# Sums of float32r products written in descending order of columns, weights at other places modulo 128 bytes

## The chip, the cores and the metric

The kernel runs on one NeuronCore of a Trainium2 chip. The time is the device time of one execution, in microseconds (us). Before the change it is 1235.84 us, the median of three runs (1231.7, 1235.84 and 1236.56). An engine is named as in the profile: PE is TensorE's matmul, PEld its weight load, DVE VectorE, ACT ScalarE, POOL GpSimd, SP the queue that issues most DMAs.

## What is computed

Two residual layers run over 512 tokens of 1024 features, in float32. Layer 0 mixes tokens with a grouped complex state-space scan (S5) and a gated unit, layer 1 with forgetting attention of 16 heads (FoX). Behind each stands a gated feed-forward layer (1024 to 2 x 2816 to 1024) with a causal convolution of width 3 on one branch. Each part is modulated by shift, scale and gate that are worked out from a conditioning vector. The change bears on the large products alone:

```python
u = h @ w_in                                  # S5, and y @ w_glu, y @ w_out
proj = h @ w_in                               # FoX: q, k, v and forget logits; o @ w_out
up = h @ w_up                                 # ConvFFN, both layers
a, b = jnp.split(up, 2, axis=-1)
return (jax.nn.silu(a_conv) * b) @ w_down
```

## The kernel before

**Layout.** Activations lie transposed: 128 features on the partitions, 512 tokens along them, eight such tiles (KT) for 1024 features. A tile of output features is 128 wide, so a product of 128 x 1024 weights with the activations is 8 steps (`k`) that add into one sum in PSUM.

**Three products for one.** Most large products are made in float32r from numbers split in two parts, `hi` (rounded by a copy on ACT, line 277) and `lo` (the rest, a subtraction on DVE, line 278). `mms` (line 294) issues three matmuls a step: hi x hi, hi x lo, lo x hi; all three times the k steps add into the same sum. The weights are the stationary operand, so each matmul has its own weight load of 128 columns, and the activations are the moving operand of 512 or 256 columns. `split` loads a tile of weights by DMA (queue of SP), makes its two parts, and `weights` hands out the k slices.

**Where weights lie.** `part_of` takes a slot of the pool and starts the weights `aside` elements of 4 bytes behind its beginning. A slot has `ROOM` = 9 x 128 elements, which is 36 x 128 bytes, so `aside` alone tells how one tile's weights lie modulo 128 bytes against another's. It is 0 by default; `ASIDE` = 16 elements is 64 bytes.

**`product`** (line 298 and on) runs over the output tiles `ms` and has three parts. The *head* makes several tiles at once, k outside, tiles inside, over `halves`: with two halves every matmul is 256 columns wide (the first tiles of both feed-forward layers, three tiles each), with one half 512 (the first four tiles of `fox`'s output product). The *middle* makes one tile after the other at 512 columns. The *tail* makes its tiles for the first half of the tokens and then for the second, 256 columns wide, with weights 64 bytes aside, so that the norm that follows can start on the first half. Each finished sum goes to `evac`, a function of the caller that reads it from PSUM: `gated` in the feed-forward layer, `add_residual` (line 362) behind w_down and the mixers' outputs, `project` (queries and keys), `glu`.

**`quarters`** (line 510 and on) replaces two tiles of `w_up` by seven products of half size in the manner of Strassen and Winograd: `times` (line 550) issues 4 k steps x 3 matmuls of 256 columns; its weights are sums and differences of blocks of `w_up`, split like the others and laid 64 bytes aside. `copy` (line 557, ACT) takes an interim sum out of PSUM, and the sums of two are made on DVE (line 518). It is used for 33 of the 44 pairs of tiles.

**`fox_values`** makes the values the other way round: tokens' activations are the stationary operand and the weights, 64 bytes aside, the moving one (line 1361), 256 columns, or 272 with the forget logits.

**What sets the order.** Each engine takes its instructions in the order in which the program issues them. PE runs through the products one behind the other; `mm` and `aux` hold four banks of PSUM each, so a sum can be read while the next is made. Weights are split ahead: five slots of `w_hi` and `w_lo`, three of `raw`. Between the products, `tick` issues pieces of the modulation of later parts (DMA of SP or POOL, reduction on DVE), and in `fox` `step=self.unit` issues pieces of attention between the k steps.

Other float32r products lie outside the functions that the change touches: `glu_head` (line 1198), the attention logits (line 1470), the weighing of values (line 1520). The S5 part's products are float32 without the split.

Of the kernel before, what the change touches and what calls it, by code (L numbers as in the profile page):

```python
# [8 lines left out]
F32 = mybir.dt.float32  # L9
F32R = mybir.dt.float32r  # L10
I32 = mybir.dt.int32
AF = mybir.ActivationFunctionType
ALU = mybir.AluOpType
# [4 lines left out]
P = 128  # L18
D = 1024
KT = D // P  # L20
S = 512
# [9 lines left out]
NH = 16  # L31
HD = 64
# [5 lines left out]
RAW, WB = 3, 5  # L38
# [23 lines left out]


ROOM, ASIDE = 9 * P, 16


def part_of(pool, shape, name, tag, bufs, aside=0):

    _, n, w = shape
    t = pool.tile([P, ROOM if bufs == WB else n * w + P], F32R, name=name, tag=tag, bufs=bufs)  # L70
    return t[:, aside:aside + n * w].rearrange("p (n w) -> p n w", w=w)


class Trunk:
# [223 lines left out]
    def product(self, w, ms, nk, x, evac, head=0, tail=0, after=None, ticks=0, halves=HALVES, tail_pool=(), first=None, step=None):  # L298


        ms = list(ms)
        full = slice(0, S)
        if head:
            wk = first or {m: self.weights(w[m], nk) for m in ms[:head]}
            ps = {m: self.mm.tile([P, S], F32, name="mmp") for m in ms[:head]}
            for c in halves:
                for k in range(nk):
                    for m in ms[:head]:
                        self.mms(ps[m][:, c], wk[m], x, k, nk, c)
                    self.finish_norm((k + 1) * head)  # L310
                    if step:
                        step(3)
            for m in ms[:head]:
                evac(m, ps[m], full)
                self.tick(ticks)
        for m in ms[head:len(ms) - tail]:
            wk = self.weights(w[m], nk)
            ps = self.mm.tile([P, S], F32, name="mmp")
            for k in range(nk):
                self.mms(ps, wk, x, k, nk, full)  # L320
                if step:
                    step()
            evac(m, ps, full)
            self.tick(ticks)
        if tail:
            last = ms[len(ms) - tail:]
            wk = {m: self.weights(w[m], nk, *tail_pool, aside=ASIDE) for m in last}
            for c in HALVES:
                for m in last:
                    if c is HALVES[1] and m == last[tail // 2]:  # L330
                        rb = self.rms_rows(y)
                    ps = self.mm.tile([P, S // 2], F32, name="mmp")
                    for k in range(nk):
                        self.mms(ps, wk[m], x, k, nk, c)
                    evac(m, ps, c)
                if c is HALVES[0]:
                    y = after[0](c)
                else:
                    y2 = after[0](c)
                    after[1](HALVES[0], y, rb)  # L340
            self.pending = lambda: after[1](HALVES[1], y2)
# [168 lines left out]
    def quarters(self, pool, l, f, x, finish):  # L510

        nc = self.nc
        H, N = KT // 2, S // 2
        t1, t2 = HALVES
        a, b = (self.raw([P, KT, P], self.io["w_up"][l][2 * f + j]) for j in range(2))
        a11, a12, a21, a22 = a[:, :H], a[:, H:], b[:, :H], b[:, H:]
        c, d = (pool.tile([P, 2, H, P], F32, name="sums", bufs=2) for _ in range(2))
        sub = lambda o, u, v, op=ALU.subtract: nc.vector.tensor_tensor(o, u, v, op)  # L518
        w = {}
        copied = self.copied  # L520

        def parts(src, names, *where):
            hi, lo = (
                pool.tile([P, H * P + P], F32R, name=n, tag="e" + n)[:, ASIDE:ASIDE + H * P].rearrange("p (n w) -> p n w", w=P)
                if where else part_of(self.wpool, [P, len(names) * H, P], n, n, WB, ASIDE)
                for n in ("w_hi", "w_lo")
            )
            with self.behind(*copied):
                self.put_parts(hi, lo, src)
            for j, n in enumerate(names):  # L530
                w[n] = hi[:, j * H:(j + 1) * H], lo[:, j * H:(j + 1) * H]
# [14 lines left out]
        def times(o, wn, xn, first=True):  # L546
            (whi, wlo), (xhi, xlo) = w[wn], xs[xn]
            for k in range(H):
                for n, (wt, xt) in enumerate(((whi, xhi), (whi, xlo), (wlo, xhi))):
                    self.last_mm = nc.tensor.matmul(  # L550
                        o, wt[:, k], xt[:, k], start=(first and k == 0 and n == 0), stop=(k == H - 1 and n == 2),
                        skip_group_check=True,
                    )

        def copy(o, last=False):
            t = self.tmp.tile([P, N], F32, name="nm_h", bufs=4)
            a = nc.scalar.activation(t, o, AF.Copy)  # L557
            if last:
                self.copied = [a.ins]
            return t  # L560
# [5 lines left out]
        c1 = copy(p1)  # L566
        times(p5, "s1", "t1")
        c5 = copy(p5)
        times(p2, "a12", "b21")
        sub(oa[:, t1], p2, c1, ALU.add)  # L570
        times(p1, "s2", "t2", False)
        c2 = copy(p1, True)
        times(p5, "s4", "b22", False)
        sub(oa[:, t2], p5, c2, ALU.add)
        finish(2 * f, oa, slice(0, S))
        times(p4, "a22", "t4")
        c4 = copy(p4)
        times(p1, "s3", "t3", False)
        sub(ob[:, t2], p1, c5, ALU.add)
        sub(ob[:, t1], p1, c4)  # L580
        finish(2 * f + 1, ob, slice(0, S))

    def ffn(self, i, l, x, nxt, ticks=0, plain=None):
# [96 lines left out]
class Ew:  # L680
# [29 lines left out]
    def sub(self, a, b, out=None):  # L710
        return self.tt(a, b, ALU.subtract, out)
# [577 lines left out]
class Kernel(S5):  # L1289
# [32 lines left out]
    def fox_values(self, pool, x):  # L1322
# [26 lines left out]
        def values(qs, blocks, w, aux=()):  # L1349
            todo = [(q, b) for q in qs for b in blocks]  # L1350
            ps = {
                k: self.aux.tile([P, S], F32, name="aux") if k in aux else self.mm.tile([P, S], F32, name="mmp")
                for k in todo
            }
            for k in range(KT):
                for q, b in todo:
                    hi, lo = w[q][k]
                    n = W if q else W + NH
                    tb = slice(b * P, (b + 1) * P)
                    for i, (xt, wt) in enumerate(((xhi, hi), (xhi, lo), (xlo, hi))):  # L1360
                        self.last_mm = nc.tensor.matmul(  # L1361
                            ps[q, b][:, :n], xt[:, k, tb], wt, start=(k == 0 and i == 0), stop=(k == KT - 1 and i == 2),
                        )
                self.finish_norm((k + 1) * len(todo))
            for q, b in todo:
                pv = ps[q, b][:, :W].rearrange("p (g r d) -> p g r d", r=2, d=HD)
                hi, lo = (self.v[:, 2 * q:2 * q + 2, b, :, t, :] for t in range(2))
                self.evac = [self.put_parts(hi, lo, pv).ins]
                if todo[0][0] == 0 and (b != 1 or q):
                    self.tick(1)  # L1370
                if q == 0:
                    nc.vector.tensor_tensor(ft[:, b, :], ps[q, b][:, W:W + NH], bf, ALU.add)

        w = load(range(2))
        self.tick(1)
# [265 lines left out]
```

## Time and profile before

| what | value |
|---|---|
| median of three runs | 1235.84 us (1231.7 to 1236.56) |
| the profiled execution | 1233.09 us |
| its span, first to last instruction | 1231.3 us |
| mean granted TensorE clock | 0.995 |
| DMA | 183.83 MB, mean 149 GB/s |
| matmuls by line 294, line 550, line 1361 | 2808, 2772, 384 |

How to read the profile: one execution was recorded by the hardware profiler. "L294 PE MATMUL mmp<-ghi,w_hi 128*128 128x512 f32 x312 | 121.8, 390" says that line 294 issued 312 matmuls with weights of 128 x 128 and a moving operand of 128 x 512, from the tiles ghi and w_hi into a sum named mmp; that PE was busy with them for 121.8 us (overlaps counted once) and that one took 390 ns on the average. Matmuls are pipelined: the next starts before the last has ended, so the distance of two starts is less than the duration. In the timeline the first column is the start in us from the span's beginning, the second the duration in us. In a row of windows the columns are the stretch, its length, then busy time and instructions of the engines (PE, PEld, DVE, ACT, POOL, or PE alone where the row is of one line's matmuls), the granted clock, the share of the DMA engines and GB/s. The chain of waits is followed back from the last instruction to whatever ended last before it.

### The profile page before, as it was taken

Reading aid. Unit: us, or ns where it says so; the run is one execution under the profiler, and the core shown is the slowest. Engines: PE = TensorE matmul, PEld = TensorE weight load, DVE = VectorE, ACT = ScalarE, POOL = GpSimd, SP = SyncE. Lnnn points to the kernel's source line nnn. Section 1 sums busy time; section 2 is a strip of 40 time slices with the busy share of each in tenths; the row PEclk is TensorE's granted clock in tenths of the full one; section 3 lists DMA queues with packets and bytes.
Section 4 is the critical chain, followed back from the end, with each engine's and each line's share of the span. In section 5 each row is a group of like instructions: output and inputs, shape, how many; then the busy total and the mean of one; then the engine's idle time right before and its main releaser. Section 6 shows DMA issues by size and latency. Waiting matters only on the chain.

```text
span 1231.3 us, 20566 instructions
## 1 busy us (share of the span) xinstructions
PE 1200.5 (97%) x7921; PEld 1031.2 (84%) x7921; DVE 1009.0 (82%) x1872; ACT 606.3 (49%) x1137; POOL 82.7 (7%) x143
## 2 busy tenths in 40 slices
PE   7999999999999999999999999999999999999997
PEld 2466678898989899889899887878989999999987
DVE  7988886779899988799687578876899887888865
ACT  3543465335544543445443565664366554545443
POOL 0000000100000000000000243430000000000000
PEclk9999999999999999999999999999999999999999
DMA  9776668530354544444445543432122332323231
GB/s 356 244 237 215 223 225 286 192 129 35 129 178 158 192 161 160 152 168 132 125 139 190 176 150 124 147 118 94 70 69 95 120 122 77 116 86 123 95 96 69
DMA packets 74385, 183.83 MB, mean 149 GB/s; under 512 B 23231, under 2 KB 25631, under 8 KB 73263
## 3 DMA queue, kind: packets, MB, share of 16 engines
q1 hardware_dynamic: 68239, 161.02, 38.4%
q0 software_dynamic: 5760, 20.97, 5.0%
q8 instruction: 62, 1.02, 0.3%
q10 hardware_dynamic: 288, 0.52, 0.1%
q14 instruction: 36, 0.29, 0.1%
HBM read 175.57 MB, written 6.92 MB: 148 GB/s over the span
## 4 chain that ended last, share of the span: by engine, by line
PE 75%; DVE 15%; DMA 4%; issue 3%; ACT 2%; POOL 0%; SPq 0%; DVEq 0%; ACTq 0%; POOLq 0%
PE mmp L294 32%; PE mmp L550 16%; PE aux L550 6%; DVE w_lo L278 5%; PE mmp L1169 4%; PE mmp L1361 2%; DMA rawd<-in_w_down 2%; PE aux L971 2%; PE mmp L1198 2%; PE aux L1060 1%; PE aux L1500 1%; PE mmp L205 1%; PE aux L1052 1%; DVE ada_raw L247 1%; PE mmp L1109 1%
## 5 line engine op out<-in xcount | busy, mean ns | idle before, releaser
L278 DVE TENSOR_TENSOR w_lo<-raw,w_hi 128x1024 fp32r<-128x1024 f32 (+4 forms) x173 | 183.3, 1065 | 35.4 <-ACT w_hi L277 34.8
L277 ACT ACTIVATE w_hi<-raw 128x1024 fp32r<-128x1024 f32 (+4 forms) x173 | 154.8, 905 | 101.5 <-PE mmp L294 53.1
L294 PE MATMUL mmp<-ghi,w_hi 128*128 128x512 f32 (+1 forms) x392 | 145.1, 370 | 0.0
L294 PE MATMUL mmp<-glo,w_hi 128*128 128x512 f32 (+1 forms) x392 | 144.8, 369 | 0.0
L294 PE MATMUL mmp<-ghi,w_lo 128*128 128x512 f32 (+1 forms) x392 | 144.5, 369 | 0.0
L294 PE MATMUL mmp<-a_hi,w_hi 128*128 128x512 f32 (+1 forms) x376 | 138.8, 372 | 1.5 <-ACT a_hi L433 1.5
L294 PE MATMUL mmp<-a_hi,w_lo 128*128 128x512 f32 (+1 forms) x376 | 136.6, 364 | 0.3 <-DVE w_lo L278 0.3
L294 PE MATMUL mmp<-a_lo,w_hi 128*128 128x512 f32 (+1 forms) x376 | 136.2, 363 | 0.0
L550 PE MATMUL mmp<-w_hi 128*128 128x256 f32 x396 | 111.4, 281 | 2.6 <-ACT nm_h L557 2.6
L550 PE MATMUL mmp<-w_hi,w_lo 128*128 128x256 f32 x396 | 111.1, 281 | 0.7 <-DVE w_lo L278 0.7
L550 PE MATMUL mmp<-w_lo,w_hi 128*128 128x256 f32 x396 | 111.1, 281 | 0.0
L557 ACT ACTIVATE nm_h<-mmp 128x256 f32<-128x256 f32 x99 | 37.9, 384 | 131.5 <-PE mmp L550 131.5
L278 DVE TENSOR_TENSOR w_lo<-sums,w_hi 128x1024 fp32r<-128x1024 f32 x74 | 90.1, 1219 | 0.3 <-ACT w_hi L277 0.2
L294 PEld LDWEIGHTS mmp<-ghi,w_lo 128*128 128x128 f32 x392 | 74.2, 189 | 12.7 <-DVE w_lo L278 0.4
L294 PEld LDWEIGHTS mmp<-glo,w_hi 128*128 128x128 f32 x392 | 74.5, 190 | 11.1
L277 ACT ACTIVATE w_hi<-sums 128x1024 fp32r<-128x1024 f32 x74 | 76.7, 1054 | 14.4 <-DVE sums L518 11.2
L294 PEld LDWEIGHTS mmp<-ghi,w_hi 128*128 128x128 f32 x392 | 74.2, 189 | 11.4
L294 PEld LDWEIGHTS mmp<-a_hi,w_hi 128*128 128x128 f32 x376 | 70.6, 189 | 13.8 <-issue 2.6
L294 PEld LDWEIGHTS mmp<-a_hi,w_lo 128*128 128x128 f32 x376 | 70.9, 189 | 12.3 <-DVE w_lo L278 1.3
L362 DVE SCALAR_TENSOR_TENSOR h<-mmp,par,h 128x512 f32<-128x512 f32 (+1 forms) x100 | 68.1, 683 | 15.3 <-PE mmp L294 15.0
L294 PEld LDWEIGHTS mmp<-a_lo,w_hi 128*128 128x128 f32 x376 | 71.1, 189 | 9.7
L550 PEld LDWEIGHTS mmp<-w_hi 128*128 128x128 f32 x396 | 74.3, 188 | 3.0 <-ACT nm_h L557 3.0
(317 smaller groups left out, 3092.6 us busy)
## 6 DMA issues: line engine op xcount, KB each, us to landing
raw<-in_w_up SPq DMA_DIRECT2D x88, 512.0 KB, 3.3
raw<-in_ada_w SPq DMA_DIRECT2D x40, 512.0 KB, 6.3
ada_raw<-in_ada_t POOLq DMA_DIRECT2D x40, 512.0 KB, 3.9
nf<-nfd SPq DMA_DIRECT2D x8, 1152.0 KB, 6.5
raw<-in_fox_qk SPq DMA_DIRECT2D x16, 512.0 KB, 3.6
raw<-in_w_down SPq DMA_DIRECT2D x24, 320.0 KB, 3.0
rawd<-in_w_down SPq DMA_DIRECT2D x24, 256.0 KB, 3.4
raw<-in_w_down SPq DMA_DIRECT2D x16, 384.0 KB, 3.3
```

Of the source, the lines that this page charges most:

```text
L205: self.last_mm = nc.tensor.matmul(ps[32 * qq:32 * qq + 32, :], self.sc32[:, k, :], w[:, q * S:(q + 1) * S], start=(step is steps[0]), stop ...
L247: nc.vector.tensor_tensor_reduce(w, w, self.c_row, 1.0, 0.0, ALU.mult, ALU.add, sums[:, j:j + 1])
L277: nc.scalar.activation(hi, src, AF.Copy)
L278: return nc.vector.tensor_tensor(lo, src, hi.bitcast(F32), ALU.subtract)
L294: self.last_mm = self.nc.tensor.matmul(o, wt, xt[:, cols], start=(k == 0 and n == 0), stop=(k == nk - 1 and n == 2),)
L362: add = self.nc.vector.scalar_tensor_tensor(self.h[:, m, cols], ps, self.par[i][:, 16 + m:17 + m], self.h[:, m, cols], op0=ALU.mult, op1=A ...
L550: self.last_mm = nc.tensor.matmul(o, wt[:, k], xt[:, k], start=(first and k == 0 and n == 0), stop=(k == H - 1 and n == 2), skip_group_che ...
L557: a = nc.scalar.activation(t, o, AF.Copy)
L971: nc.tensor.matmul(ps[g2][:, j, cols], x[rows, a + j, r].rearrange("p c j -> p (c j)"), self.rr[rows, planes, q, :], start=(j == 0 and r = ...
L1169: nc.tensor.matmul(ps, w[m][:, k, :], x[:, k], start=(k == 0), stop=(k == KT - 1))
L1198: nc.tensor.matmul(gps[m], wt, xt[:, k], start=(k == 0 and part == 0 and xt is yhi), stop=(k == KT - 1 and part == 1))
L1361: self.last_mm = nc.tensor.matmul(ps[q, b][:, :n], xt[:, k, tb], wt, start=(k == 0 and i == 0), stop=(k == KT - 1 and i == 2),)
```

## The change

`back` gives a view of a sum's columns from the last to the first. The matmuls now write through that view: the first column of the moving operand goes to the last column of the PSUM tile, the second to the one before, and so on. Every reader of such a sum reads it through the same view. It is done for the middle and the tail of `product`, for its head if there are two halves, for `quarters` and for `fox_values`. The head with one half (in `fox`) and the products outside these functions stay as they were. The moving operands and the weights are read in the old order.

`PLACES` are eight distances in elements: 4, 8, 16, 32, 48, 64, 80 and 96 bytes. The middle of `product` takes the one of its output tile's number modulo 8 (it was 0), `quarters` that of its pair's number modulo 8 (it was 64 bytes, and stays so for the one block that has a slot of its own). The head with two halves goes from 0 to 64 bytes.

```diff
--- before.py
+++ after.py
@@ -62,6 +62,7 @@
 
 
 ROOM, ASIDE = 9 * P, 16
+PLACES = (1, 2, 4, 8, 12, 16, 20, 24)
 
 
 def part_of(pool, shape, name, tag, bufs, aside=0):
@@ -69,6 +70,11 @@
     _, n, w = shape
     t = pool.tile([P, ROOM if bufs == WB else n * w + P], F32R, name=name, tag=tag, bufs=bufs)
     return t[:, aside:aside + n * w].rearrange("p (n w) -> p n w", w=w)
+
+
+def back(t):
+
+    return t[:, ::-1]
 
 
 class Trunk:
@@ -301,8 +307,11 @@
         ms = list(ms)
         full = slice(0, S)
         if head:
-            wk = first or {m: self.weights(w[m], nk) for m in ms[:head]}
+            two = len(halves) == 2
+            wk = first or {m: self.weights(w[m], nk, aside=ASIDE if two else 0) for m in ms[:head]}
             ps = {m: self.mm.tile([P, S], F32, name="mmp") for m in ms[:head]}
+            if two:
+                ps = {m: back(t) for m, t in ps.items()}
             for c in halves:
                 for k in range(nk):
                     for m in ms[:head]:
@@ -314,8 +323,8 @@
                 evac(m, ps[m], full)
                 self.tick(ticks)
         for m in ms[head:len(ms) - tail]:
-            wk = self.weights(w[m], nk)
-            ps = self.mm.tile([P, S], F32, name="mmp")
+            wk = self.weights(w[m], nk, aside=PLACES[m % 8])
+            ps = back(self.mm.tile([P, S], F32, name="mmp"))
             for k in range(nk):
                 self.mms(ps, wk, x, k, nk, full)
                 if step:
@@ -331,8 +340,8 @@
                         rb = self.rms_rows(y)
                     ps = self.mm.tile([P, S // 2], F32, name="mmp")
                     for k in range(nk):
-                        self.mms(ps, wk[m], x, k, nk, c)
-                    evac(m, ps, c)
+                        self.mms(back(ps), wk[m], x, k, nk, c)
+                    evac(m, back(ps), c)
                 if c is HALVES[0]:
                     y = after[0](c)
                 else:
@@ -522,7 +531,7 @@
         def parts(src, names, *where):
             hi, lo = (
                 pool.tile([P, H * P + P], F32R, name=n, tag="e" + n)[:, ASIDE:ASIDE + H * P].rearrange("p (n w) -> p n w", w=P)
-                if where else part_of(self.wpool, [P, len(names) * H, P], n, n, WB, ASIDE)
+                if where else part_of(self.wpool, [P, len(names) * H, P], n, n, WB, PLACES[f % 8])
                 for n in ("w_hi", "w_lo")
             )
             with self.behind(*copied):
@@ -548,13 +557,13 @@
             for k in range(H):
                 for n, (wt, xt) in enumerate(((whi, xhi), (whi, xlo), (wlo, xhi))):
                     self.last_mm = nc.tensor.matmul(
-                        o, wt[:, k], xt[:, k], start=(first and k == 0 and n == 0), stop=(k == H - 1 and n == 2),
+                        back(o), wt[:, k], xt[:, k], start=(first and k == 0 and n == 0), stop=(k == H - 1 and n == 2),
                         skip_group_check=True,
                     )
 
         def copy(o, last=False):
             t = self.tmp.tile([P, N], F32, name="nm_h", bufs=4)
-            a = nc.scalar.activation(t, o, AF.Copy)
+            a = nc.scalar.activation(t, back(o), AF.Copy)
             if last:
                 self.copied = [a.ins]
             return t
@@ -567,17 +576,17 @@
         times(p5, "s1", "t1")
         c5 = copy(p5)
         times(p2, "a12", "b21")
-        sub(oa[:, t1], p2, c1, ALU.add)
+        sub(oa[:, t1], back(p2), c1, ALU.add)
         times(p1, "s2", "t2", False)
         c2 = copy(p1, True)
         times(p5, "s4", "b22", False)
-        sub(oa[:, t2], p5, c2, ALU.add)
+        sub(oa[:, t2], back(p5), c2, ALU.add)
         finish(2 * f, oa, slice(0, S))
         times(p4, "a22", "t4")
         c4 = copy(p4)
         times(p1, "s3", "t3", False)
-        sub(ob[:, t2], p1, c5, ALU.add)
-        sub(ob[:, t1], p1, c4)
+        sub(ob[:, t2], back(p1), c5, ALU.add)
+        sub(ob[:, t1], back(p1), c4)
         finish(2 * f + 1, ob, slice(0, S))
 
     def ffn(self, i, l, x, nxt, ticks=0, plain=None):
@@ -1359,17 +1368,18 @@
                     tb = slice(b * P, (b + 1) * P)
                     for i, (xt, wt) in enumerate(((xhi, hi), (xhi, lo), (xlo, hi))):
                         self.last_mm = nc.tensor.matmul(
-                            ps[q, b][:, :n], xt[:, k, tb], wt, start=(k == 0 and i == 0), stop=(k == KT - 1 and i == 2),
+                            back(ps[q, b][:, :n]), xt[:, k, tb], wt, start=(k == 0 and i == 0), stop=(k == KT - 1 and i == 2),
                         )
                 self.finish_norm((k + 1) * len(todo))
             for q, b in todo:
-                pv = ps[q, b][:, :W].rearrange("p (g r d) -> p g r d", r=2, d=HD)
+                sums = back(ps[q, b][:, :W if q else W + NH])
+                pv = sums[:, :W].rearrange("p (g r d) -> p g r d", r=2, d=HD)
                 hi, lo = (self.v[:, 2 * q:2 * q + 2, b, :, t, :] for t in range(2))
                 self.evac = [self.put_parts(hi, lo, pv).ins]
                 if todo[0][0] == 0 and (b != 1 or q):
                     self.tick(1)
                 if q == 0:
-                    nc.vector.tensor_tensor(ft[:, b, :], ps[q, b][:, W:W + NH], bf, ALU.add)
+                    nc.vector.tensor_tensor(ft[:, b, :], sums[:, W:W + NH], bf, ALU.add)
 
         w = load(range(2))
         self.tick(1)
```

## What the change does to the time: the prediction

> **What bounds the kernel now.** I read the page first, its busy shares and its chain, and then the starts of consecutive products in the timeline.
>
> ```profile
> span 1231.3 us, 20566 instructions
> PE 1200.5 (97%) x7921; PEld 1031.2 (84%) x7921; DVE 1009.0 (82%) x1872; ACT 606.3 (49%) x1137; POOL 82.7 (7%) x143
> PE 75%; DVE 15%; DMA 4%; issue 3%; ACT 2%; POOL 0%; SPq 0%; DVEq 0%; ACTq 0%; POOLq 0%
> PE mmp L294 32%; PE mmp L550 16%; PE aux L550 6%; DVE w_lo L278 5%; PE mmp L1169 4%; PE mmp L1361 2%; DMA rawd<-in_w_down 2%; PE aux L971 2%; PE mmp L1198 2%; PE aux L1060 1%; PE aux L1500 1%; PE mmp L205 1%; PE aux L1052 1%; DVE ada_raw L247 1%; PE mmp L1109 1%
> ```
>
> TensorE makes 75% of the chain, and lines 294, 550 and 1361, which the change touches, make 56%. So what counts is how far apart two products start, and not the mean duration of one, which holds a tail that the next product overlaps. The timeline gives the distance: here are the first and the last row of stretches without a stall.
>
> ```profile
> 294.96 0.39 PE L294 MATMUL mmp<-a_hi,w_lo 128*128 128x512 f32 x1
> ...
> 297.91 0.39 PE L294 MATMUL mmp<-a_hi,w_hi 128*128 128x512 f32 x1
> ...
> 269.72 0.28 PE L294 MATMUL mmp<-a_hi,w_hi 128*128 128x256 f32 x1
> ...
> 272.48 0.28 PE L294 MATMUL mmp<-a_hi,w_lo 128*128 128x256 f32 x1
> ...
> 469.67 0.28 PE L550 MATMUL mmp<-w_hi 128*128 128x256 f32 x1
> ...
> 473.91 0.28 PE L550 MATMUL mmp<-w_hi 128*128 128x256 f32 x1
> ...
> 619.66 0.28 PE L294 MATMUL mmp<-ghi,w_hi 128*128 128x256 f32 x1
> ...
> 623.28 0.28 PE L294 MATMUL mmp<-ghi,w_lo 128*128 128x256 f32 x1
> ```
>
> The first pair spans 13 steps of 512 columns: 2.95/13 = 226.9 ns. The other pairs are 256 columns wide. Line 294 in the head of `product`, weights at place 0: 23 steps, 2.76/23 = 120.0 ns. Line 550 in `quarters`, weights 64 bytes aside: 36 steps, 4.24/36 = 117.8 ns. Line 294 in the tail, 64 bytes aside too: 32 steps, 3.62/32 = 113.1 ns. The last two have the same place and different distances, so place is not the only thing that sets them; but no stretch at place 0 in this head settles under 120.
>
> A second reading tells what part of this is TensorE's own pace. The granted clock falls to half for a moment (0.50, third figure from the right in the first row below), and there the distance is:
>
> ```profile
> 615.90:617.00 1.10, 1.10 (x8) 1.10 (x6) 0.00 (x0) 1.10 (x2) 0.00 (x0) 0.50 0.00 0
> ...
> 617.87 0.41 PE L294 MATMUL mmp<-ghi,w_lo 128*128 128x256 f32 x1
> ...
> 618.94 0.39 PE L294 MATMUL mmp<-glo,w_hi 128*128 128x256 f32 x1
> ```
>
> Five steps, 1.07/5 = 214 ns for 256 columns: 0.836 ns a column. Were the pace TensorE's alone, the full clock would give half of that, 107 ns for 256 and 214 for 512. The rows show 113 to 120 and 227. So **some 6% of every product is lost to something that does not slow with TensorE's clock**: a store that is read or written. The trace does not say which: the moving operand, the weights (both SBUF) or the sums (PSUM).
>
> **The change part by part.** It adds, removes and moves no instruction, no DMA and no wait; each of its edits changes an address pattern. The products that it touches:
>
> ```profile
> L294 PE MATMUL mmp<-ghi,w_hi 128*128 128x512 f32 x312 | 121.8, 390 | 0.0
> ...
> L294 PE MATMUL mmp<-zhi,w_lo 128*128 128x512 f32 x48 | 18.7, 389 | 0.0
> 0.00:1231.00 1231.00, 584.49 (x2808) 1.00 0.44 149
> 0.00:1231.00 1231.00, 332.68 (x2772) 1.00 0.44 149
> 0.00:1231.00 1231.00, 46.31 (x384) 1.00 0.44 149
> ```
>
> The three last rows are all products of lines 294, 550 and 1361. Of line 294's 2808, the groups kept apart by shape (the first and the last of eleven rows of 512 columns into `mm` stand above; three more into `aux` have 8 each) give 2064 + 24 of 512 columns; 96 of these are the head of `fox` (one half, not touched) and 24 are the fifth glu tile (not in `product`). That leaves 1968 of 512 columns, at 227 ns 447 us, and 720 + 2772 + 384 = 3876 of about 256, at 118 ns 457 us: **904 us of a span of 1231 hang on the distance**, 1% of it being 9 us.
>
> *Sums written backwards.* Nothing in this trace is written by TensorE with a negative step, so the price is bounded from both sides. From below: if the 6% is lost where the sums are written, and direction is its cause, the distances fall to 214 and 107 ns: 1968 x 13 + 3876 x 11 ns = 68 us saved. From above: if sums that do not ascend go in one column at a time at the slow pace of 0.836 ns a column, 512 columns take 428 ns and 256 take 214: 1968 x 201 + 3876 x 96 ns = 768 us lost. I take zero, for two reasons in the rows. Weights moved by 64 bytes change the distance, so the loss reacts to an SBUF address, and that says reading more than writing. And the moving operand is still read forwards: SBUF sees the old order.
>
> The Trainium skill, page "PSUM — Partial Sum Buffer", section "Specifications (TRN2)", speaks against the change: PSUM has 8-byte lines and any access pattern that isn't contiguous slows matmuls significantly. Page "Advanced Engine Details and Errata", section "Memory Cachelines", words it as every two consecutive elements being contiguous, and by that wording a backward pair still shares a line. No row here shows a backward or strided sum of any width; by the first wording the upper bound above would hold, by the second the zero.
>
> *Readers of the sums.* ACT and DVE now read PSUM backwards. The nearest rows are a PSUM read in steps of eight elements and one in order, both 128x512 on ACT:
>
> ```profile
> L1171 ACT ACTIVATE uf<-mmp 128x512 f32<-128x512 f32 x7 | 4.2, 603 | 10.7 <-issue 10.6
> L1420 ACT ACTIVATE hi<-mmp 128x512 fp32r<-128x512 f32 x8 | 4.6, 579 | 0.0
> L557 ACT ACTIVATE nm_h<-mmp 128x256 f32<-128x256 f32 x99 | 37.9, 384 | 131.5 <-PE mmp L550 131.5
> L557 ACT ACTIVATE nm_h<-aux 128x256 f32<-128x256 f32 x33 | 12.1, 368 | 1.7 <-PE aux L550 1.5
> PE mmp L550 <- ACT nm_h L557: 2.6, 2, 2.4
> ```
>
> A step of eight costs 603 - 579 = 24 ns. From zero to 24 ns on each of line 557's 132 copies (99 + 33) is 0 to 3 us of ACT, which is 49% busy, and PE waits for that line 2 times in all, 2.6 us. I take 0, for DVE's reads too, of which no row has a step: four banks of `mm` and the next product cover it. Without that cover it would be 3 us.
>
> *Places.* Weights of `product`'s middle tiles go from place 0 to eight places from 4 to 96 bytes, those of `quarters` from 64 bytes to the same eight, the head in two halves from 0 to 64. Bounds for `quarters` are the rows above: 113.1 (gain 4.7) to 120.0 (loss 2.2) from 117.8, times 2772: -13 to +6 us. At 512 columns a settled stretch has 226.9; behind a switch from 256 to 512 columns, stretches like this one are slower for six products:
>
> ```profile
> 443.24 0.40 PE L294 MATMUL mmp<-ghi,w_hi 128*128 128x512 f32 x1
> ...
> 444.40 0.39 PE L294 MATMUL mmp<-ghi,w_lo 128*128 128x512 f32 x1
> ```
>
> Five steps, 1.16/5 = 232 ns. If a place held the 512-wide products there, each would lose 5 ns: 1968 x 5 = +10 us at most; the least is 0. I take half of `quarters`' tiles at 120 and half unchanged, 1386 x 2.2 ns = +3 us, since two of the eight places (4 and 8 bytes) lie nearest to 0 and the others between, and 0 for the 512-wide ones, because they settled at 226.9 while their weights lay at 0, where the 256-wide head has its worst distance. The head in two halves gains 2.2 ns on 288 products (3 tiles, 8 steps, 3 products, 2 halves, 2 layers): -0.6 us.
>
> **Sum.** 0 + 0 + 3 - 0.6 = +2.4 us on the profiled execution of 1233.1 us (span 1231.3 and 1.8 around it). That execution was 2.7 us under the median of 1235.84, so against the median the forecast is **1238 us**: no change that a measurement shows. What it can tell apart from none is about 0.5%, 6 us.
>
> **Rivals.**
>
> *The backward order removes the loss: faster.* For it: the 6% does not follow TensorE's clock, and the sum's order is the one thing changed in all touched products. Against it: the place of weights moves the distance too. Price: up to 68 us. But 107 ns needs weight loads to keep up; the nearest row is a run of 64-column products, each with a load of 128 columns:
>
> ```profile
> 174.79 0.94 PE L1052 MATMUL aux<-u,t 128*128 128x64 f32 x7
> 175.54 0.48 PE L1198 MATMUL mmp<-a_hi,w_hi 128*128 128x512 f32 x1
> ...
> 307.00:500.00 193.00, 192.41 (x1250) 175.27 (x1249) 174.10 (x270) 92.34 (x147) 11.68 (x22) 1.00 0.46 159
> ```
>
> Seven in 0.75 us is 107 ns, so loads just keep up. The stretch from 307 to 500 us has DVE at 174 of 193 us: with PE 11 us shorter (845 x 11 and 405 x 13 ns would be 15 us) DVE begins to be late with `w_lo` and `sums`. I count 70% of the gain: -47 us, **1190 us**, between 1172 and 1215.
>
> *The places hold the products in their slow patterns: slower.* Place: the settled stretches of lines 294 and 550. Price: +10 us (512 columns at 232 ns) and +6 us (256 at 120): **1252 us**, and up to 1270 if places off the grid of 16 bytes cost as much again. It decides from the point where six of eight places act like place 0. For it: the 120 ns row. Against it: 512-wide products return to 226.9 after six.
>
> *Sums go in one column at a time: much slower.* The price is the upper bound, 768 us, on 1236: **some 2000 us**, less what hides behind it. For it speaks that TensorE's writes in this trace all ascend without a step, so nothing shows that another order keeps the pace. Against it: backward neighbours are as near as forward ones. The skill's first wording, above, is this rival.
>
> **How the numbers follow.** No change in the pace, 1238 us with its own range of 1224 to 1250 (the -13 and +6 of `quarters`, the +10): 0.37. The loss goes away, 1190: 0.29. Places slow, 1252: 0.14. One column at a time, 2000: 0.20. The range leaves out the last alone and takes in the ends of the others: 1172 to 1270. Faster by over 0.5% (under 1229.7) takes the second case and 0.07 of the first: 0.36. Slower (over 1242) takes the third and fourth and 0.13 of the first: 0.47. Within: 0.17.
>
> **What would show it.** Right: 226.9 ns steady in `product`'s 512-wide tiles whatever the place, 113 to 120 in `quarters` with the distance changing from one tile to the next by its place, line 557 at 384 ns and the same instruction counts. The first rival shows as 214 to 220 ns at 512 columns and under 112 at 256, while the head of `fox`, which stays forward, keeps 227. The second shows as 232 ns that does not settle. The third shows as over 400 ns a product of 512 columns, and PE near 100% with DVE under 60%. I am wrong if the loss sits where the sums are written.

## The result: 0.6% slower, and the profile after

The changed kernel takes **1240.97 us** (median of five runs, 1240.0 to 1245.38), the kernel before on the same chip 1233.84 us (median of five, 1231.7 to 1236.56). The ratio is **1.006 [1.004, 1.008]**: 7.4 us, between 5 and 10. The forecast was 1238 us, in a range of 1172 to 1270. The number lies near the forecast; but the forecast was "no change that a measurement shows", and this change is clear of the noise. One of its terms failed, as the traces show.

The page of the changed kernel, its first lines and its chain of waits:

```profile
span 1243.6 us, 20566 instructions
PE 1214.8 (98%) x7921; PEld 1034.7 (83%) x7921; DVE 1009.2 (81%) x1872; ACT 605.6 (49%) x1137; POOL 82.4 (7%) x143
PE 64%; issue 18%; DVE 11%; DMA 4%; ACT 1%; POOL 1%; SPq 0%; DVEq 0%; POOLq 0%; ACTq 0%
```

The same instructions, PE busy for 14 us longer, DVE, ACT and POOL as before: no engine does more, one is slower at the same work. The chain gives less to PE and more to "issue" (time for which it found no wait), together 82% against 78%; that is no new wait, since the list of PE's waits has the same lines with nearly the same sizes.

This execution took 1245.38 us, the longest of its five. Some 6 us of its distance to before are lost in the first 197 us, ahead of the first product that the change touches (at 209.7 us). Here is that stretch, of the kernel before and then of the changed one:

```profile
0.00:197.00 197.00, 187.12 (x1354) 116.83 (x1355) 161.04 (x368) 89.41 (x234) 2.60 (x22) 0.99 0.75 256
```

```profile
0.00:197.00 197.00, 187.07 (x1328) 115.23 (x1329) 159.78 (x367) 88.16 (x233) 2.59 (x22) 0.96 0.73 246
```

26 matmuls fewer are done by then, at a clock of 0.96 against 0.99. The experiments below have from 0.95 (E2) to 0.99 (E3, E6, E7, E10) there, with and without the change's edits, so this varies from one execution to the next. The size of an effect is therefore read below from the sums by line and the distances, and its verdict from the times.

Where PE's time went is in the groups by line and shape, of the kernel before and then of the changed one (lines 294, 550, 557 and 1361 are now 300, 559, 566 and 1370; columns as in the prediction, which shows the first row of before, 390 ns):

```profile
L294 PE MATMUL mmp<-a_hi,w_hi 128*128 128x512 f32 x280 | 111.9, 400 | 0.0
L550 PE MATMUL mmp<-w_lo,w_hi 128*128 128x256 f32 x396 | 111.1, 281 | 0.0
L550 PE MATMUL aux<-w_hi 128*128 128x256 f32 x132 | 37.0, 280 | 0.0
```

```profile
L300 PE MATMUL mmp<-ghi,w_hi 128*128 128x512 f32 x312 | 123.2, 395 | 0.0
L300 PE MATMUL mmp<-a_hi,w_hi 128*128 128x512 f32 x280 | 113.3, 405 | 0.0
L559 PE MATMUL mmp<-w_lo,w_hi 128*128 128x256 f32 x396 | 111.0, 280 | 0.0
L559 PE MATMUL aux<-w_hi 128*128 128x256 f32 x132 | 36.7, 278 | 0.0
```

The 512-wide products of `product`'s middle take 5 ns longer on the average (390 to 395, 400 to 405); the 256-wide ones of `quarters` shown take 1 to 2 ns less. The sums of all products of lines 300, 559 and 1370 say the same:

```profile
0.00:1246.00 1246.00, 593.65 (x2808) 0.99 0.44 148
0.00:1246.00 1246.00, 331.36 (x2772) 0.99 0.44 148
0.00:1246.00 1246.00, 47.09 (x384) 0.99 0.44 148
```

Against 584.49, 332.68 and 46.31 before: +9.2, -1.3 and +0.8 us. The distances tell which tiles. First and last starts of seven stretches of the changed kernel, from its timeline; the place is that of the tile's weights modulo 128 bytes:

```profile
435.48 0.40 PE L300 MATMUL mmp<-ghi,w_hi 128*128 128x512 f32 x1
...
438.28 0.39 PE L300 MATMUL mmp<-ghi,w_hi 128*128 128x512 f32 x1
...
453.71 0.40 PE L300 MATMUL mmp<-ghi,w_hi 128*128 128x512 f32 x1
...
456.28 0.39 PE L300 MATMUL mmp<-ghi,w_lo 128*128 128x512 f32 x1
...
469.90 0.39 PE L300 MATMUL mmp<-ghi,w_hi 128*128 128x512 f32 x1
...
473.13 0.39 PE L300 MATMUL mmp<-ghi,w_lo 128*128 128x512 f32 x1
...
441.08 0.28 PE L559 MATMUL mmp<-a_hi,w_hi 128*128 128x256 f32 x1
...
448.03 0.28 PE L559 MATMUL mmp<-a_hi,w_lo 128*128 128x256 f32 x1
...
448.14 0.28 PE L559 MATMUL aux<-w_hi 128*128 128x256 f32 x1
...
449.39 0.28 PE L559 MATMUL aux<-w_hi,w_lo 128*128 128x256 f32 x1
...
456.51 0.28 PE L559 MATMUL mmp<-a_hi,w_hi 128*128 128x256 f32 x1
...
466.29 0.28 PE L559 MATMUL mmp<-w_hi,w_lo 128*128 128x256 f32 x1
...
839.19 0.39 PE L300 MATMUL mmp<-v,w_hi 128*128 128x512 f32 x1
...
841.46 0.39 PE L300 MATMUL mmp<-v,w_lo 128*128 128x512 f32 x1
```

At 512 columns: 48 bytes, 12 steps, 2.80/12 = 233 ns; 96 bytes, 11 steps, 2.57/11 = 234; 8 bytes, 14 steps, 3.23/14 = 231. None returns to 226.9. The head of `fox`, whose sums are still written forwards and whose weights lie at 0, keeps it: 10 steps, 2.27/10 = 227. At 256 columns: 48 bytes, 59 steps, 6.95/59 = 117.8; 64 bytes, 11 steps, 1.25/11 = 113.6, and, 8 us later at the same place, 83 steps, 9.78/83 = 117.8. The profile does not say whether direction or place did this, since the change moves both in the same products.

The readers stand where they stood:

```profile
L566 ACT ACTIVATE nm_h<-mmp 128x256 f32<-128x256 f32 x99 | 37.8, 383 | 134.2 <-PE mmp L559 134.0
L566 ACT ACTIVATE nm_h<-aux 128x256 f32<-128x256 f32 x33 | 12.1, 366 | 1.7 <-PE aux L559 1.6
```

### The profile page after: what moved, and what is told of

It is laid out like the page before. It is cut to its first block, busy times and chain, and to the rows that moved or that the text cites. A ratio compares the mean times of both kernels' runs of the same rounds, so it can differ in the third digit from the quotient of the medians.

```text
span 1243.6 us, 20566 instructions
## 1 busy us (share of the span) xinstructions
PE 1214.8 (98%) x7921; PEld 1034.7 (83%) x7921; DVE 1009.2 (81%) x1872; ACT 605.6 (49%) x1137; POOL 82.4 (7%) x143
## 4 chain that ended last, share of the span: by engine, by line
PE 64%; issue 18%; DVE 11%; DMA 4%; ACT 1%; POOL 1%; SPq 0%; DVEq 0%; POOLq 0%; ACTq 0%
PE mmp L300 26%; PE mmp L559 12%; PE aux L559 5%; PE mmp L1178 4%; DVE w_lo L284 3%; PE mmp L1370 2%; PE aux L980 2%; DMA rawd<-in_w_down 2%; PE mmp L1207 2%; PE aux L1069 1%; PE aux L1510 1%; PE aux L1061 1%; PE mmp L211 1%; DVE ada_raw L253 1%; DMA ada_raw<-in_ada_t 1%
```

## The experiments

**The theory** after the result: the order in which sums are written costs nothing; the place of a tile's weights sets a repeating pattern of distances, and 0 is the best of the places used for 512 columns. **Its rival**: the backward order costs the 5 ns, and the places do little. Times are given as ratios to the kernel before on the same chip with a 95% interval, or, for a single run, beside the median of that chip's runs of it. Distances "settled" are means over the starts of all products of one width, order and place, stalls left out; the tile's number gives the place, the trace the starts.

### E1: the backward order alone

All of the change's backward sums; weights at the places of before.

```diff
-            wk = self.weights(w[m], nk, aside=PLACES[m % 8])
+            wk = self.weights(w[m], nk)
...
-                if where else part_of(self.wpool, [P, len(names) * H, P], n, n, WB, PLACES[f % 8])
+                if where else part_of(self.wpool, [P, len(names) * H, P], n, n, WB, ASIDE)
```

(and the head with two halves back at 0)

> The order alone: sums written backwards as in the change, weights at their old places (0 in the middle and the head of product, 64 bytes in quarters). Theory A, the backward order is what slows the products of 512 columns: starts 232 to 234 ns apart at place 0 too, as in the change, and about +8 to +10 us on the kernel before, less what 256 columns gain (quarters at 64 bytes 115.0 instead of 117.4 ns, some -6 us). Theory B, the new places slow them: 227 ns as before, and a kernel 5 to 8 us faster than before through the 256-wide products.

Measured: 0.9994 [0.9971, 1.0017]. From this run a group, the sums of lines 300 and 559, and first and last start of 39 steps of the middle:

```profile
L300 PE MATMUL mmp<-ghi,w_hi 128*128 128x512 f32 x312 | 121.8, 390 | 0.0
```

```profile
0.00:1246.00 1246.00, 583.59 (x2808) 0.99 0.45 148
0.00:1246.00 1246.00, 334.35 (x2772) 0.99 0.45 148
```

```profile
429.78 0.39 PE L300 MATMUL mmp<-a_hi,w_lo 128*128 128x512 f32 x1
...
438.62 0.39 PE L300 MATMUL mmp<-ghi,w_lo 128*128 128x512 f32 x1
```

8.84/39 = 226.7 ns, and 390 ns a product, as before. Settled over the whole kernel: 227.56 backwards here, 227.58 forwards before. Direction costs nothing, and gains nothing: the 5 to 8 us that theory B counted on from the 256-wide products did not come either (line 559 334.35 us, before 332.68). The rival falls.

### E2: the places alone

```diff
 def back(t):
 
-    return t[:, ::-1]
+    return t
```

> The places alone: sums written forwards, weights at the eight places of the change, the head in two halves at 64 bytes. Theory A: 512-wide products 227 ns apart at every place, and the time within 3 us of before. Theory B: 231 to 234 ns at the places of 4 to 96 bytes, and 8 to 10 us more than before. In quarters, 113 to 120 ns by place under both.

Measured: 1.0024 [1.0002, 1.0046]. The same two views, lines 300 and 559:

```profile
L300 PE MATMUL mmp<-ghi,w_hi 128*128 128x512 f32 x312 | 123.2, 395 | 0.0
```

```profile
0.00:1246.00 1246.00, 590.91 (x2808) 0.99 0.45 148
0.00:1246.00 1246.00, 332.07 (x2772) 0.99 0.45 148
```

The 395 ns are back without a single backward sum. Settled distances in ns, by place in bytes, of E2 and of the changed kernel:

| place | 4 | 8 | 16 | 32 | 48 | 64 | 80 | 96 |
|---|---|---|---|---|---|---|---|---|
| 512 columns, E2 (forwards) | 232.2 | 230.8 | 232.0 | 233.0 | 232.9 | 233.2 | 231.8 | 233.9 |
| 512 columns, the change (backwards) | 232.3 | 230.8 | 232.9 | 233.0 | 233.0 | 233.2 | 231.8 | 233.9 |
| 256 columns, E2 | 118.2 | 115.6 | 118.4 | 118.4 | 118.0 | 115.2 | 118.8 | 117.9 |
| 256 columns, the change | 118.2 | 115.7 | 118.4 | 118.4 | 118.0 | 115.1 | 118.8 | 118.0 |

Place sets the distance, to 0.1 ns but for one, whatever the order. E2's time lies lower than the change's 1.006, though, and than the 8 to 10 us that were expected (0.2 to 5.7 by its interval): against E1's trace its lines lose 7.3 us (300), and win 2.3 (559) and 0.6 (1370), so 4.4 us are due, and the two medians of this chip, 1241.67 and 1239.61, lie 2.1 apart. The intervals of both ratios meet at 1.004 to 1.005; the runs don't tell whether order adds a microsecond or two to place; E1's interval leaves it 2 us at most.

### E3: backward in the 256-wide products alone

512-wide sums and values forwards, all places as before except the head, which has 64 bytes. One of the edited lines:

```diff
-            ps = back(self.mm.tile([P, S], F32, name="mmp"))
+            ps = self.mm.tile([P, S], F32, name="mmp")
```

> Backward order only in the products of 256 columns (quarters, the head in two halves, the tail), all at 64 bytes; the products of 512 columns forwards at place 0, the values forwards. Theory A and B alike: 227 ns at 512 columns, 115 ns in quarters and the tail against 117.4 and 116.9 before, 115 in the head against 120: some 2772 x 2.4 + 416 x 1.6 + 288 x 4.6 ns = 8.6 us faster than before, if the 115 ns of the change at 64 bytes come from the order. If they come from the neighbourhood of other places (a pattern carried over from one tile to the next), the time is that of before within 3 us.

Measured: 0.9999 [0.9977, 1.0022]; 117.29 ns settled at 64 bytes, where the change had 115.1 at that place. So the change's faster 64-byte tiles owe nothing to the order; they stand behind tiles at other places (E10 returns to this).

### E4: the moving operand read backwards too

E1, with the moving operand of the middle and of `quarters` read from the last column to the first, so that the sums come out in their natural order.

```diff
-                o, wt, xt[:, cols], start=(k == 0 and n == 0), stop=(k == nk - 1 and n == 2),
+                o, wt, turn(xt[:, cols]), start=(k == 0 and n == 0), stop=(k == nk - 1 and n == 2),
...
-                self.mms(ps, wk, x, k, nk, full)
+                self.mms(back(ps), wk, x, k, nk, full, back)
```

> As the run with the order alone, but in the middle of product and in quarters the moving operand is read backwards as well, so that read and write go the same way and the sums lie in the natural order. If the direction of the write against PSUM is what counts, the distances are those of the order alone. If opposite directions of reading and writing count, 512-wide products are 227 ns apart. If reading backwards meets the weight loads otherwise, 256-wide products leave the range of 113 to 120 ns.

Measured: one run of 1245.11 us, beside 1238.94. The middle, weights at 0, 38 steps:

```profile
429.65 0.40 PE L300 MATMUL mmp<-a_hi,w_hi 128*128 128x512 f32 x1
...
438.52 0.40 PE L300 MATMUL mmp<-ghi,w_lo 128*128 128x512 f32 x1
```

8.87/38 = 233.4 ns, as at the bad places; settled, 233.4 against E1's 227.56. Writing backwards is free, reading backwards costs some 6 ns a product here, which none of the three cases named beforehand had. At 512 columns the loss belongs to the side that reads. `quarters`, with its moving operand turned round as well, shows nothing of it: 117.8 ns settled against E1's 117.5, line 559 333.71 us against 334.35. Its products differ from the middle's in width and in place (64 bytes), and no run tells which of the two spares them.

### E5: one moving column for all

The kernel before; the middle reads the first column of its moving operand 512 times (the function in the last place is applied to it in `mms`).

```diff
-                self.mms(ps, wk, x, k, nk, full)
+                self.mms(ps, wk, x, k, nk, full, lambda t: t[:, 0:1].to_broadcast([P, S]))
```

> The kernel before, but in the middle of product the moving operand is its first column read 512 times (step 0), so every column of those sums is alike and the outputs are not the reference's. Instructions, weights and sums are the same. If the 6% at 512 columns come from reading the moving operand from place to place in SBUF, or from its meeting with the weight load, starts are 214 to 217 ns apart instead of 227. If they come from writing the sums, 227 ns stays.

Measured: one run of 1232.51 us, beside 1239.15. Twenty steps of the middle, the sum of line 294, and the wait that cost PE most:

```profile
429.68 0.38 PE L294 MATMUL mmp<-ghi,w_hi 128*128 128x512 f32 x1
...
434.00 0.38 PE L294 MATMUL mmp<-ghi,w_lo 128*128 128x512 f32 x1
```

```profile
0.00:1246.00 1246.00, 566.74 (x2808) 0.98 0.45 148
```

```profile
PE mmp L294 <- DVE w_lo L278: 8.0, 5, 3.3
```

4.32/20 = **216.0 ns**: all but 2 of the 13 ns that "do not slow with TensorE's clock" are gone when the moving operand needs no new data, at weights and sums as before. So the loss comes with fetching the moving operand from ever new addresses; whether by itself or by its meeting with the weight load, which the expectation names together, this run does not tell. (The Trainium skill, page "TensorE: Matmul & The Clock Gate", section "Back-to-back issue gap", puts the gap of a lone product at its columns at 2.4 GHz and 2.5 ns more, by estimate 215.8 ns for 512; only this run comes there, the kernel's own products stay 11 ns above it.) Of the 17.8 us less on line 294 a single run shows 6.6: PE now waits 8.0 us for `w_lo`, as the prediction's first rival had foreseen for a faster PE, and the clock of this execution was 0.985.

### E6: eight other places

E2 with other distances.

```diff
-PLACES = (1, 2, 4, 8, 12, 16, 20, 24)
+PLACES = (3, 6, 10, 14, 18, 22, 26, 30)
```

> As the run with the places alone, with eight other places: 12, 24, 40, 56, 72, 88, 104 and 120 bytes. If only the distance from place 0 in bytes counts, the 512-wide products take 230 to 234 ns at all of them, as at the first eight, and none is under 227; the 256-wide ones 113 to 120. If multiples of 16 bytes are what is slow (8 bytes gave 230.8 ns and 115.7, the least of the small places), then 24, 40, 56, 72, 88, 104 and 120 all give 231 and 115 to 116, and 12 bytes 232 and 118 like 4 bytes.

Measured: one run of 1242.61 us, beside 1239.15; line 300 has 593.48 us. Settled, in ns:

| place | 12 | 24 | 40 | 56 | 72 | 88 | 104 | 120 |
|---|---|---|---|---|---|---|---|---|
| 512 columns | 230.2 | 231.1 | 233.0 | 233.0 | 233.3 | 233.4 | 233.1 | **227.5** |
| 256 columns | 116.9 | 120.2 | 119.1 | 117.8 | 118.4 | **114.1** | 118.4 | 119.4 |

Of the 17 places seen, 512-wide products have two good ones, 0 and 120 bytes, side by side on the circle of 128; 256-wide ones have theirs elsewhere: 88, then 8 (and 64, where it falls into the faster of two patterns, see E10). What is good for one width is bad for the other (88: 233.4 and 114.1; 120: 227.5 and 119.4). There is no slope from near to far. Not all of these places were run alone: for 512 columns only 0 was, for 256 columns 64, 8 and 88 (0 in the head); the rest are seen with other places before and behind them.

### E7 and E9: 256-wide products at 8 and at 88 bytes

The kernel before, with `quarters`, the head of two halves and the tail at one place, 8 bytes (NEAR = 2) or 88 bytes (NEAR = 22); the middle stays at 0 and everything is written forwards.

```diff
-            wk = first or {m: self.weights(w[m], nk) for m in ms[:head]}
+            wk = first or {m: self.weights(w[m], nk, aside=NEAR if len(halves) == 2 else 0) for m in ms[:head]}
...
-            wk = {m: self.weights(w[m], nk, *tail_pool, aside=ASIDE) for m in last}
+            wk = {m: self.weights(w[m], nk, *tail_pool, aside=NEAR) for m in last}
...
-                if where else part_of(self.wpool, [P, len(names) * H, P], n, n, WB, ASIDE)
+                if where else part_of(self.wpool, [P, len(names) * H, P], n, n, WB, NEAR)
```

> The kernel before with forward sums, 512-wide products at place 0, and every 256-wide one (quarters, the head in two halves, the tail) at 8 bytes instead of 64, 0 and 64. If a place has its own pattern whatever came before, 115.6 ns: 2772 x 1.8 + 416 x 1.2 + 288 x 4.2 ns = 6.7 us faster than before (0.5%). If the pattern depends on what came before, and 115.6 arises only behind products at other places, 117 to 120 ns and the time of before within 2 us.

> As the run with 8 bytes, but every 256-wide product at 88 bytes. Beside other places 88 bytes settled at 114.1 ns. If that is the place's own pattern: 2772 x 3.3 + 416 x 2.7 + 288 x 5.7 ns = 11.9 us faster than before (1.0%). If it hangs on the neighbours, like the two patterns at 64 bytes, 117 to 118 ns and the time of before within 3 us. 227 ns at 512 columns under both.

Measured: 8 bytes 0.9954 [0.9928, 0.998], settled at 115.7 (6.7 us less were expected; 5.7 show, 2.5 to 8.9); 88 bytes **0.9946 [0.992, 0.9971]**, settled at 113.9. At 88 bytes, the sums of lines 294 and 550, and a stretch of `quarters`:

```profile
0.00:1246.00 1246.00, 581.39 (x2808) 0.99 0.45 148
0.00:1246.00 1246.00, 324.66 (x2772) 0.99 0.45 148
```

```profile
441.07 0.28 PE L550 MATMUL mmp<-w_hi 128*128 128x256 f32 x1
...
442.32 0.28 PE L550 MATMUL mmp<-w_hi,w_lo 128*128 128x256 f32 x1
```

1.25/11 = 113.6 ns. Line 550 wins 8.0 us and line 294 3.1; 6.7 us show in the time (3.6 to 9.9), where 11.9 were expected. This version beats both kernels, with each width of product at a place of its own.

### E8: sums in pairs far apart

The kernel before; the middle's moving operand is read in its old order (the first function only gives it the same shape), and its sums are written pair by pair into every second pair of columns, first the even pairs and then the odd ones, so that pairs written one after the other start 16 bytes apart.

```diff
-                self.mms(ps, wk, x, k, nk, full)
+                self.mms(ps, wk, x, k, nk, full, lambda t: t.rearrange("p (j n c) -> p j n c", j=2, c=2), lambda t: t.rearrange("p (n j c) -> p j n c", j=2, c=2))
```

> The kernel before, but in the middle of product each two neighbouring columns of a sum are written together and the next two four columns on (first the even pairs, then the odd ones), so tokens of those sums are permuted and the outputs are not the reference's. If any access pattern of the sum that isn't contiguous slows a matmul, 512-wide products are well over 232 ns apart, up to 428. If two neighbours are enough, or the order of writing does not count at all, 227 ns stays.

Measured: one run of 1241.45 us, beside 1239.15. Thirty-nine steps:

```profile
429.72 0.39 PE L294 MATMUL mmp<-a_hi,w_lo 128*128 128x512 f32 x1
...
438.56 0.39 PE L294 MATMUL mmp<-ghi,w_lo 128*128 128x512 f32 x1
```

8.84/39 = 226.7 ns, no different (settled over the whole kernel: 227.6). The Trainium skill, page "PSUM — Partial Sum Buffer", section "Specifications (TRN2)", has any pattern that isn't contiguous slow matmuls significantly; neither descending sums (E1) nor pairs with gaps show any of it in float32r. Pairs of neighbours were kept in both, as the Trainium skill, page "Advanced Engine Details and Errata", section "Memory Cachelines", asks; a step of two, which would break the pairs, was not tried.

### E10: one column of weights for all

The kernel before; the weight load of the middle reads the first of its columns 128 times (here the function is applied to the weights).

```diff
-                self.mms(ps, wk, x, k, nk, full)
+                self.mms(ps, wk, x, k, nk, full, lambda t: t[:, 0:1].to_broadcast([P, P]))
```

> The kernel before, but in the middle of product each weight load reads one column 128 times (step 0), so the outputs are not the reference's; moving operand and sums as before. If the 227 ns at place 0 are the moving operand meeting the weight load, 214 to 217 ns as with one moving column. If the moving operand's own reading sets them, 227 ns stays; what the places add (up to 234) would then be the only part that comes from the meeting.

Measured: one run of 1229.56 us, beside 1237.01. Four starts, and one 13 steps behind the first; then the sum of line 550:

```profile
443.40 0.39 PE L294 MATMUL mmp<-ghi,w_hi 128*128 128x512 f32 x1
443.62 0.40 PE L294 MATMUL mmp<-glo,w_hi 128*128 128x512 f32 x1
443.86 0.40 PE L294 MATMUL mmp<-ghi,w_lo 128*128 128x512 f32 x1
444.09 0.39 PE L294 MATMUL mmp<-ghi,w_hi 128*128 128x512 f32 x1
...
446.40 0.40 PE L294 MATMUL mmp<-glo,w_hi 128*128 128x512 f32 x1
```

```profile
0.00:1246.00 1246.00, 324.27 (x2772) 0.99 0.45 148
```

3.00/13 = 230.8 ns, here in a cycle of 226, 234, 234; settled over the whole kernel, 231. Neither of the two values expected (214 to 217, or 227) came. With next to no new data in the weight load the loss stays, and almost no distance falls under 225 (26 of some 1845). So the 11 ns over E5's 216 do not come from the load's fetching new columns. That they are the moving operand's own, with no part of the load in them, is argued and not shown, since the loads still run beside it; and what a load reads does count, for this one made the middle 3.5 ns slower.

A by-catch: line 550, not touched here, has 324.27 us against 332.68. Its weights lie at 64 bytes as before, but now settle at 113.9 instead of 117.4. This place has **two patterns**, 113.3 and 117.8 (both are in the changed kernel's rows above, which read 113.6 and 117.8 in hundredths of a us), and a stretch mostly keeps the one it is in. Of the 33 pairs of `quarters`, by the median of their first 24 distances, 2 begin in the fast one in the kernel before, in E1 and in E3 and 3 in E8, but 15 in E5 and 31 here, where the middle alone was edited: so what ran before weighs on which one a stretch falls into. By what step it does so no run shows. That is why a single place's mean moves between runs (115.1, 116.7, 117.3, 117.4).

### E11: the change with the middle back at 0

```diff
-            wk = self.weights(w[m], nk, aside=PLACES[m % 8])
+            wk = self.weights(w[m], nk)
```

> The change with one part undone: the middle of product at place 0 again; sums still backwards, quarters at the eight places, the head in two halves at 64 bytes. If the middle's places are the whole loss, 227.6 ns at 512 columns, 1968 x 5.0 ns = 9.8 us less than the change, so 0 to 4 us faster than before. If the backward order or the places of quarters cost as well, the time stays above that of before.

Measured: 1.0001 [0.9976, 1.0026]; settled at 227.7 with 512 columns. The group and the sum of line 300:

```profile
L300 PE MATMUL mmp<-ghi,w_hi 128*128 128x512 f32 x312 | 121.9, 391 | 0.0
```

```profile
0.00:1246.00 1246.00, 582.64 (x2808) 0.99 0.45 148
```

One edit undone, and the loss is gone, with all sums backwards and `quarters` at its eight places. From both sides, E2 and E11, the loss is the middle's places: by the distances all of it, by the times to within some 3 us, which is what the two intervals leave open.

## Why the prediction was right in its number and wrong in one step

- **What bounds the kernel: right.** The starts of the products set the time. 5 ns on 1968 of them is the change's result.
- **Sums written backwards, taken at 0 between -68 and +768 us: right**, and for the reason given, that the loss reacts to the reading side (E1 for the price, E4 and E5 for the side). "I am wrong if the loss sits where the sums are written": it does not.
- **The readers, taken at 0 of up to 3 us: right.** Line 557's copies went from 384 to 383 ns and from 368 to 366.
- **`quarters` at eight places, +3 us, and the head, -0.6: wrong sign in the first, within its bounds.** The distances of all 256-wide products but the values, each from the start before it and waits included, add up to 422.8 us after 424.7: -1.9 with head and tail. The reason, that places near 0 behave like 0, fell: 8 bytes is one of the best (115.7), and 64 bytes fell into its fast pattern more often. The values, for which the prediction has no term, moved by +0.5 us, and not through the order: E11, backwards too, has them at 115.2 and E9, forwards, at 117.5, the change at 117.7 after 114.8.
- **The step that failed: "0 for the 512-wide ones, because they settled at 226.9 while their weights lay at 0, where the 256-wide head has its worst distance".** It carried a ranking of places from one width to the other. All eight places give 231 to 234 ns; of the seventeen seen in these runs, 0 is the best together with 120 bytes. The term measured some +9 us (distances of the middle, added up in the same way, 451.5 us after 442.7; line 300's sum +9.2), near the upper bound that the prediction had worked out as +10 from the row of 232 ns behind a switch of width.
- **The sum**: 8.9 - 1.9 + 0.5 = +7.5 us, measured 7.4; with one execution traced of each kernel, that is closer than the evidence can bear. The forecast's +2.4 was 5 us short. That 1238 lies within 3 us of 1240.97 is in part luck: two misses, +9 and some -4, partly cancel, and the forecast stands on a median of before that is 2 us above the one measured beside the change. What the traces show is therefore what the prediction wrote for its second rival, *the places hold the products in their slow patterns*: 232 ns that does not settle, with that rival's +10 us but without its +6. It had a chance of 0.14, and "no change in the pace" 0.37.
- **The loss goes away (1190 us)** fell with E1, and **one column at a time (2000 us)** with E1 and E8. As to the first, E5 shows what a cure for the loss would bring: 17.8 us less of line 294, of which a single run showed a third. Two of its rows were read too kindly. The 6% is the 512-wide products' loss; 113 to 120 ns against 107 is 6 to 12%. And "loads just keep up" with 107 ns is not what the run of 64-column products shows: its steady starts lie 111 to 112 ns apart, and only the last step, to the next line's product, is shorter (84).

What stays open: which part of the reading makes the periodic patterns, why 0 and 120 bytes suit 512 columns and 88 and 8 suit 256, whether it is the weights' place itself that counts or their distance from the moving operand's, which no run moved, and whether 226.7 ns is the moving operand's pace with no weight load beside it at all; no run here was without loads.

## What to carry to other kernels

Where products run back to back, measure the distance of starts for each width and each place of the weights separately, and do not carry a ranking from one width to another; a mean over a kernel hides patterns of 113 and 118 ns at one and the same place. An edit that moves two things in the same instructions, here order and place, needs one run for each before its time means anything. The order in which a matmul's sums are written can be chosen freely, as far as these runs go (descending, and pairs with gaps); the order in which the moving operand is read cannot, at 512 columns.

## What the runs showed of the hardware that was not expected

- float32r sums written in descending order, or in pairs 16 bytes apart, cost nothing: 227.6 ns settled for 512 columns in both, as forwards (E1, E8).
- Reading the moving operand in descending order costs some 6 ns of 227.6 at 512 columns (233.4, E4), and nothing in the 256-wide products of `quarters` (117.8 against 117.5); reading one column 512 times saves 11 (216.0, E5).
- Where the weights lie modulo 128 bytes moves a product by up to 6 ns of 227.5 at 512 columns (233.9 at 96 bytes) and by up to 6 of 113.9 at 256 (120.2 at 24 bytes). A weight load that reads one column over and over, at place 0, makes the distance longer, not shorter (231, E10).
- One place can hold two steady patterns (113.3 and 117.8 ns at 64 bytes), and which one a stretch falls into went with what ran before it (2 of 33 pairs began in the fast one in the kernel before, 31 in E10).
